# Mixing the streams of a two-layer decoder by finer steps

## Chip, core and metric

The kernel runs on one core of a Trainium2 chip, in one launch. The metric is device time in microseconds (us). Five engines run their own instruction queues side by side: TensorE (PE) multiplies matrices, VectorE (DVE) and ScalarE (ACT) do elementwise work, GpSimd (POOL) adds a few sums of weights, and SyncE (SP) issues nearly all transfers. An instruction starts when those before it on its engine have been issued and the semaphores that it waits for have been reached.

## What is computed

One step of a decoder with two layers, in fp32, for 1024 prompt tokens and 8 sample tokens that share all weights:

```python
for l in range(DEPTH):                       # DEPTH = 2, D_MODEL = 1024, D_FF = 2816
    hn = rmsnorm(h, g[0])
    if l < N_A:                              # layer 0: gated recurrence + memory attention
        mix, S = a_mixer(hn, w_in_a[l], lbs[l], hg_norm[l], mem_k[l], mem_v[l], w_o[l], hg_s0[l])
    else:                                    # layer 1: stick-breaking attention + memory attention
        mix = b_mixer(hn, w_in_b[l - N_A], ..., k_all, v_all, q_pos, k_pos, mem_k[l], mem_v[l], w_o[l])
    h = h + rmsnorm(mix, g[1])
    h = h + rmsnorm(swiglu(rmsnorm(h, g[2]), w_gu[l], w_down[l]), g[3])
    if l == N_A - 1:                         # shared keys and values, after layer 0
        sb_k, sb_v = jnp.split(rmsnorm(h, g_kv) @ w_kv, 2, axis=-1)
```

The samples bring their own recurrent states, paged keys and values, and memory caches; the new states, keys and values are outputs too.

## The kernel before

**Groups and layout.** The tokens are worked in two groups: group 0 has 512 prompt tokens, group 1 has the other 512 and the 8 samples. Activations lie with the features on the partitions and the tokens along the rows, so a projection (`proj`, L212 on) is 8 blocks of 128 features by 512 or 2 x 260 tokens.

**Products in three passes.** A weight tile of 128 x 512 is loaded by SP (L203), its high half is rounded by ACT (L208) and its low half is the difference, taken by DVE (L209). Each 128 x 128 block then takes three matmuls in this order: high weight by high activation, high by low, low by high. So the first two need ACT alone and the third needs DVE. A projection is 48 matmuls (L222) for group 0, twice as many of 260 columns for group 1. `split[0]` always names the last weight split on DVE, and `with tc.issue_after(ins)` keeps what is issued under it behind `ins` on its engine.

**Order.** The program is written as generators, each a stream of steps. `weave((stream, n), ...)` takes the next step from the stream whose count of steps divided by its weight `n` is the smallest; `drain` runs streams to their end. The Tile framework then places each engine's instructions by this order as far as its own scheduling keeps it, and inserts the waits. A stream that waits holds its engine's queue, and all that stands behind it there.

**Buffers.** `mmp` has two pairs of PSUM banks for projections: L247 (first operation of a silu), L414 (adding a partial output to the residual rows) and L818 (gate by up) on DVE free them. `wraw` has 5 raw weight tiles, `wspl` 5 split ones, `cpool` 4 tiles of 128 x 1024, `bpool` 7 of 128 x 512, `apool` 8 of 2 x 520.

**Streams that the change touches.**
- `normed` (L279 on) multiplies the residual rows by the norm, ties each row behind `split[0]`, and splits it. `residual` (L371 on) does the same with a post norm, adds the row of the residual stream and stores it; its first operation (L395) has no tie.
- `kv_proj` projects the shared keys and values; `rows_proj` makes those rows of group 0 that have tokens on the partitions.
- `hgrn_sample` (L1221 on) updates the recurrent states of the samples. It first turns the new values into rows and stores them in DRAM (`vd`), then takes one head a step: it loads the state, broadcasts that head's value rows from `vd` to all partitions (L1239), multiplies and adds (L1253 on), stores the state (L1255), multiplies by the query and sums over partitions by a matmul with `selr` (L1261). In the end the rows go to DRAM and back (`od`, L1269 and L1271) and are transposed (L1274).
- `sample_scores` (L1035 on) takes one sample a step: it loads the keys, broadcasts the query (L1054), multiplies (L1056) and reduces (L1057). `sample_pv` (L1062 on) likewise weights the values (L1077), adds two halves (L1078) and sums them over partitions by a matmul (L1068). Both serve the memory attention (`mem_attn_sample`, transposes L1124 and L1134) and stick-breaking (`sb_sample`).
- Stick-breaking for the prompt makes scores (L1500), runs scans on DVE (L1520), exponentials on ACT (L1523), transposes (L1529) and products with the values (L1540).
- The feed-forward has a plain form (`ffn`, by `proj`) and one by sums of weight quarters (`ffn_w`, L504 and L578, down projection L750 and L782), whose sums of weights (L558 to L565) come from DVE or from sums made ahead (`weight_sums`). Its slices come in parts of 5, 6, 5 and so on. With few free buffers, it takes the raw weight tiles for part 1 from `apool` (L538), where the residual rows of the last output projection lay; `token_rows` (L481) is the last to read those rows, for group 1.

Of the kernel before, what the change touches and what calls it, by code (L numbers as in the profile page):

```python
# [9 lines left out]
F32 = mybir.dt.float32  # L10
# [4 lines left out]
ALU = mybir.AluOpType  # L15
# [8 lines left out]
def tile_decoder(  # L24
# [354 lines left out]
    def residual(g, R, rstd, gc, store, acc=None, first=False):  # L379
        n = NG[g]  # L380
        w = D // 2 if first else n
        ht = [xpool.tile([P, 2, w], F32, tag=f"x{g}", name=nm("ht")) for _ in range(ND // 2)]
        for j in range(ND // 2):
            if first:
                t0 = g * G + j * P
                nc.sync.dma_start(ht[j].rearrange("p a n -> p (a n)"), x_prompt[0, t0 : t0 + P, :])
            else:
                nc.sync.dma_start(ht[j], hs[g][:, 2 * j : 2 * j + 2, :n])
        for k in range(ND):
            if first:  # L390
# [4 lines left out]
            nc.vector.scalar_tensor_tensor(R[k][:, :n], R[k][:, :n], gc(k), rstd[:, :n], op0=ALU.mult, op1=ALU.mult)  # L395
# [263 lines left out]
    class ffn_w:  # L659
# [44 lines left out]
        def part(self, pi):  # L704
# [94 lines left out]
    class ffn:  # L799
# [4 lines left out]
        def part(self, pi, own_silu=False):  # L804
# [5 lines left out]
            for j in range(nf):  # L810
# [225 lines left out]
    def sample_scores(q, load, sc):  # L1036
# [14 lines left out]
        for b in range(NB):  # L1051
# [3 lines left out]
            with tc.issue_after(split[0].ins):  # L1055
                nc.vector.tensor_mul(kt, kt, qb.unsqueeze(1).to_broadcast([P, 2, 512]))  # L1056
            nc.vector.tensor_reduce(  # L1057
                scv[:, :, :, b], kt.rearrange("p k (h d) -> p k h d", h=H), axis=AX.X, op=ALU.add
            )
            yield  # L1060

    def sample_pv(pT, load, xo, k0):  # L1062
# [10 lines left out]
        for b in range(NB):  # L1073
# [4 lines left out]
            nc.vector.tensor_add(vt[:, 0, :], vt[:, 0, :], vt[:, 1, :])  # L1078
# [7 lines left out]
        nc.vector.tensor_copy(ot[:NB, :], po[:NB, :])  # L1086
        pr = S()
# [30 lines left out]
    def mem_attn_sample(l, qm, xo):  # L1118
        HB = H * NB
        sc = small([P, 2 * HB], tag="sc", bufs=2)  # L1120
        yield from sample_scores(qm, mem_loader(cache_mem_k, l), sc)
        pr = S()
# [8 lines left out]
        nc.vector.tensor_scalar(pe[:HB, :NM], pe[:HB, :NM], sm[:HB, 0:1], None, op0=ALU.mult)  # L1131
        pb = S()
# [29 lines left out]
    def rows_proj(W, m0, xt, dst):  # L1162

        pb = [mmp.tile([P, 2, 512], F32, tag="mm", name=nm("mm")) for _ in range(2)]
        for k in range(ND):
# [4 lines left out]
            nc.vector.tensor_sub(ws[:, 1, :], raw, ws[:, 0, :].bitcast(F32))  # L1170
# [50 lines left out]
    def hgrn_sample(Ft, Kt, Qt, vs):  # L1221
# [5 lines left out]
        vd = tc.dram_tile([NB, 512], F32, name=nm("vd"))  # L1227
        nc.sync.dma_start(vd, vT[:NB, :])
        yield
        HB = H * NB  # L1230
# [13 lines left out]
        po = S()  # L1244
        for h in range(H):
# [9 lines left out]
            nc.sync.dma_start(st_sample[0, :, h].rearrange("b k v -> k b v"), stv)  # L1255
            nc.vector.tensor_mul(vbv, stv, col(Qt))
            for a in range(2):
                qs = B(F32R), B(F32R)
                split_to(qs, vb[:, a, :])
                for i, p in enumerate(qs):  # L1260
                    nc.tensor.matmul(  # L1261
                        po[:NB, :], selr[:, 2 * h + a, :], p,
                        start=(h == 0 and a == 0 and i == 0), stop=(h == H - 1 and a == 1 and i == 1),
                    )
            yield
        rows = B()
# [4 lines left out]
        nc.sync.dma_start(ot[:NB, :].rearrange("p (h v) -> p h v", v=P), od.rearrange("h b v -> b h v"))  # L1271
        pr = S()
# [112 lines left out]
    class mixer_a:  # L1385
# [12 lines left out]

        def sample(self):
            yield from hgrn_sample(self.F, self.K, self.Q, self.vs)  # L1400
# [31 lines left out]
    def kv_proj(g, xt):  # L1432
        ks = small([P, 2, H, NB], tag="ks", bufs=1) if g else None
        for j, (out, scr) in enumerate(((sbk_prompt, ksc), (sbv_prompt, vsc))):
            if j and not g:
                rows = [C(), C()]
                yield from rows_proj(w_kv, H * P, xt, rows)
# [24 lines left out]
            for h in range(H):  # L1462
# [106 lines left out]
    def sb_sample(Qs, xo):  # L1569
# [6 lines left out]
        softplus(zb, e, 2 * HB)  # L1576
        cu = S()
# [160 lines left out]
    weave((chain(a1.merge(), a1.mem()), 30), (a1.mem_sample(), 50), (rest(), 24))  # L1738
# [6 lines left out]
    drain(kv_proj(0, xk0))  # L1745
    weave((normed(0, f0.R, f0.r, lambda k: gcol(1, 0, k), xb0), 8), (o1.mm(a1.xo, 7, ND), 1))
# [5 lines left out]
    weave((chain(b0.sb(), b0.mem()), 25), (chain(fw.part(0), fw.part(1)), 18))  # L1752
# [3 lines left out]
    drain(fw.part(3), islice(p4, 4))  # L1756
# [9 lines left out]
    drain(kv_proj(1, xk1))  # L1766
    weave((normed(1, f1.R, f1.r, lambda k: gcol(1, 0, k), xb1), 8), (o0.mm(b0.xo, 7, ND), 1))
# [6 lines left out]
        (chain(b1.sb(), b1.mem()), 40), (chain(b1.sb_sample(), b1.mem_sample()), 39),  # L1774
        (chain(f0.part(0), f0.part(1), f0.part(2), islice(p3, 4)), 30),
# [40 lines left out]
```

## Time and profile before

| | us |
|---|---|
| median of 3 runs | 2419.17 |
| lowest and highest | 2416.83, 2419.40 |
| the profiled execution's own time | 2418.61 |
| its span from first to last instruction | 2416.9 |
| mean granted clock of TensorE in it | 0.999 |

All views below are of that profiled execution. A line such as `PE mm L222 <- DVE t L247: 2.0, 1, 2.0` reads: TensorE's instructions of line 222 that write `mm` waited for DVE's line 247, which writes `t`, for 2.0 us in total, once, 2.0 at the longest. A line of the timeline gives the start, the length to the end of the last of the group, engine, line, operation, output and inputs, shape, count, and in brackets the idle time before it and what ended it. A group of instructions gives count, then busy time, mean duration of one in ns, and idle time before. Matmuls are pipelined, so that their records overlap; what a matmul costs in a row of them is the distance of two starts. "PEld" is the loading of weights, "SPq" the issue of transfers, and the clock is a share of the full one.

### The profile page before, as it was taken

The numbers are of one execution on the slowest core, as the hardware profiler recorded it, in microseconds if no ns is written. First come the engines' busy times: TensorE is split into PE (matmuls) and PEld (weight loads), VectorE is DVE, ScalarE is ACT, GpSimd is POOL, SyncE is SP. The second block draws the span as 40 slices with busy tenths as digits, with TensorE's granted clock in tenths as the row PEclk, the third lists the DMA queues.
The fourth block names the chain that finished last, engine by engine and source line by source line (L and its number), as shares of the span: only waits on it lengthen the run. The fifth ranks groups of instructions, "written<-read, shape, count | busy, mean of one in ns | idle before, by whom it ended". The sixth has DMA issues, their size and how long they took to land. (4 is left out here: it accounts for less than half of the span.)

```text
span 2416.9 us, 41637 instructions
## 1 busy us (share of the span) xinstructions
PE 2384.9 (99%) x15719; PEld 2147.6 (89%) x15719; DVE 1716.2 (71%) x3154; ACT 1271.7 (53%) x2517; POOL 101.9 (4%) x155
## 2 busy tenths in 40 slices
PE   8999999999999999999999999999999999999998
PEld 6888988888779998999999989877777988999998
DVE  5867557675797676878565777788778467776876
ACT  5547544354445554666544554555455446554445
POOL 1000201110000000000000100021000000000000
PEclk9999999999999999999999999999999999999999
DMA  6454766567645447332555546454353243343321
GB/s 190 121 167 118 170 188 158 134 185 195 188 131 152 146 141 218 118 112 76 170 162 150 173 145 190 151 158 150 111 157 120 83 127 118 113 129 100 109 84 67
DMA packets 494987, 342.86 MB, mean 142 GB/s; under 512 B 19469, under 2 KB 446586, under 8 KB 494786
## 3 DMA queue, kind: packets, MB, share of 16 engines
q1 hardware_dynamic: 482242, 306.63, 42.6%
q0 software_dynamic: 12544, 33.56, 5.9%
q8 instruction: 124, 2.03, 0.3%
q14 instruction: 77, 0.63, 0.1%
HBM read 308.18 MB, written 57.10 MB: 151 GB/s over the span
## 5 line engine op out<-in xcount | busy, mean ns | idle before, releaser
L222 PE MATMUL mm<-x,ws 128*128 128x512 f32 (+1 forms) x5208 | 967.9, 343 | 4.5 <-DVE t L247 2.0
L222 PEld LDWEIGHTS mm<-x,ws 128*128 128x128 f32 x5208 | 811.3, 188 | 124.2 <-issue 2.9
L208 ACT CAST ws<-w 128x512 fp32r<-128x512 f32 x612 | 357.5, 586 | 455.8 <-PE mm L222 280.3
L209 DVE TENSOR_TENSOR ws<-w,ws 128x512 fp32r<-128x512 f32 x612 | 392.2, 646 | 246.8 <-ACT ws L208 239.5
L750 PE MATMUL q<-m,ws 128*128 128x260 f32 (+1 forms) x2304 | 282.8, 283 | 0.5 <-ACT m L229 0.3
L750 PEld LDWEIGHTS q<-m,ws 128*128 128x128 f32 x2304 | 277.3, 188 | 2.6 <-ACT m L229 0.8
L578 PE MATMUL q<-y,ws 128*128 128x260 f32 x1824 | 237.5, 284 | 0.7 <-ACT q L585 0.4
L578 PEld LDWEIGHTS q<-y,ws 128*128 128x128 f32 x1824 | 226.0, 188 | 1.9 <-ACT q L589 0.9
L222 PE MATMUL mm<-m,ws 128*128 128x512 f32 x864 | 215.6, 401 | 0.4 <-DVE r L414 0.4
L578 PE MATMUL q<-x,ws 128*128 128x260 f32 (+1 forms) x1548 | 202.9, 283 | 0.0
L222 PEld LDWEIGHTS mm<-m,ws 128*128 128x128 f32 x864 | 160.8, 189 | 36.8 <-DVE r L414 0.7
L578 PEld LDWEIGHTS q<-x,ws 128*128 128x128 f32 x1548 | 192.6, 188 | 0.1
L571 ACT CAST ws<-w 128x512 fp32r<-128x512 f32 x188 | 113.0, 618 | 87.1 <-PE q L750 27.3
L573 DVE TENSOR_TENSOR ws<-w,ws 128x512 fp32r<-128x512 f32 x188 | 126.4, 688 | 37.9 <-ACT ws L571 36.3
L504 PE MATMUL q<-x,ws 128*128 128x260 f32 (+1 forms) x720 | 90.4, 284 | 0.0
L759 DVE TENSOR_TENSOR r<-r,q 128x260 f32<-128x260 f32 (+1 forms) x144 | 54.6, 421 | 48.1 <-PE q L750 47.9
L504 PEld LDWEIGHTS q<-x,ws 128*128 128x128 f32 x720 | 87.8, 188 | 1.0 <-DVE ws L209 0.2
L229 ACT CAST m<-t 128x512 fp32r<-128x512 f32 (+1 forms) x88 | 54.8, 623 | 30.6 <-DVE t L618 15.2
L230 DVE TENSOR_TENSOR m<-t,m 128x512 fp32r<-128x512 f32 (+1 forms) x88 | 60.7, 690 | 12.8 <-ACT m L229 12.1
L277 DVE TENSOR_TENSOR st<-st,n 128x512 f32<-128x512 f32 (+1 forms) x91 | 62.3, 692 | 2.8 <-ACT n L276 1.9
L571 ACT CAST ws<-b 128x512 fp32r<-128x512 f32 x68 | 41.9, 620 | 37.1 <-PE q L750 13.8
L247 DVE TENSOR_SCALAR t<-mm 128x512 f32<-128x512 f32 (+1 forms) x48 | 33.1, 689 | 36.8 <-PE mm L222 36.8
(405 smaller groups left out, 3045.9 us busy)
## 6 DMA issues: line engine op xcount, KB each, us to landing
w<-in_w_gu SPq DMA_DIRECT2D x290, 256.0 KB
w<-in_w_down SPq DMA_DIRECT2D x160, 256.0 KB
w<-in_w_in_a SPq DMA_DIRECT2D x80, 256.0 KB
wsum<-in_w_gu POOLq DMA_DIRECT2D x36, 512.0 KB, 6.3
w<-in_w_o SPq DMA_DIRECT2D x64, 256.0 KB
w<-wsum SPq DMA_DIRECT2D x36, 256.0 KB
w<-in_w_mem_kv SPq DMA_DIRECT2D x32, 256.0 KB
c<-in_cache_mem_k SPq DMA_DIRECT2D x16, 512.0 KB
```

Source lines behind the costliest of these rows:

```text
L208: nc.scalar.copy(ws[:, 0, :n, :], raw[:, :n, :])
L209: split[0] = nc.vector.tensor_sub(ws[:, 1, :n, :], raw[:, :n, :], ws[:, 0, :n, :].bitcast(F32))
L222: nc.tensor.matmul(ps[:, a, : PW[g]], wt, xt[k][:, xi, o : o + PW[g]], start=(k == 0 and wi == 0), stop=(k == nk - 1 and wi == 2),)
L229: nc.scalar.copy(dst[0], src)
L230: nc.vector.tensor_sub(dst[1], src, dst[0].bitcast(F32))
L277: nc.vector.tensor_add(acc[:, :n], acc[:, :n], t[:, :n])
L504: ins = nc.tensor.matmul(pp[a][:, :h], wt, xt[k][:, xi, a * h : (a + 1) * h], start=(k == 0 and wi == 0), stop=(k == ND - 1 and wi == 2),)
L571: nc.scalar.copy(w[:, 0, :], src)
L573: split[0] = nc.vector.tensor_sub(w[:, 1, :], src, w[:, 0, :].bitcast(F32))
L578: nc.tensor.matmul(ps[:, :h], w[:, wj, k * P : (k + 1) * P], x[:, xi, :], start=(first and k == 0 and wi == 0), stop=(k == 3 and wi == 2), ...
L750: nc.tensor.matmul(pp[a][:, :h], wt, mids[k][:, xi, a * h : (a + 1) * h], start=(k == 0 and wi == 0), stop=(k == nf - 1 and wi == 2),)
L759: nc.vector.tensor_add(d, d, pp[a][:, :h])
```

## The change

No matmul, no transfer and no elementwise operation is added or left out; streams are cut into other steps, some instructions are tied behind others, some issue later, and the weights of the mixes follow the new counts of steps.

```diff
-    def normed(g, R, rstd, gc, out, keep=False):
+    def normed(g, R, rstd, gc, out, keep=False, behind=()):
...
-            with tc.issue_after(split[0].ins):
+            with tc.issue_after(behind[k] if behind else split[0].ins):
                 nc.vector.scalar_tensor_tensor(t[:, :n], R[k][:, :n], gc(k), rstd[:, :n], ...)
@@ residual @@
-            nc.vector.scalar_tensor_tensor(R[k][:, :n], R[k][:, :n], gc(k), rstd[:, :n], ...)
+            with tc.issue_after(split[0].ins):
+                nc.vector.scalar_tensor_tensor(R[k][:, :n], R[k][:, :n], gc(k), rstd[:, :n], ...)
@@ ffn_w.part @@
                     if late:
                         drain(late)
-                        yield
+                    yield
                     next(slice_)
                     late = slice_
-                    continue
                 yield
@@ ffn.part @@
+                yield
                 pu = proj(g, w_gu[l], 0, ND, DFF + (f0 + j) * P, self.xt)
@@ sample_scores @@
-            nc.vector.tensor_reduce(scv[:, :, :, b], ...)
+            yield
+            with tc.issue_after(split[0].ins):
+                nc.vector.tensor_reduce(scv[:, :, :, b], ...)
@@ sample_pv @@
-            nc.vector.tensor_add(vt[:, 0, :], vt[:, 0, :], vt[:, 1, :])
+            yield
+            with tc.issue_after(split[0].ins):
+                nc.vector.tensor_add(vt[:, 0, :], vt[:, 0, :], vt[:, 1, :])
...
         nc.vector.tensor_copy(ot[:NB, :], po[:NB, :])
+        yield
         pr = S()
@@ mem_attn_sample @@
         yield from sample_scores(qm, mem_loader(cache_mem_k, l), sc)
+        yield
         pr = S()
...
+        yield
         pb = S()
@@ rows_proj(W, m0, xt, dst, done=None) @@
-            nc.vector.tensor_sub(ws[:, 1, :], raw, ws[:, 0, :].bitcast(F32))
+            split[0] = nc.vector.tensor_sub(ws[:, 1, :], raw, ws[:, 0, :].bitcast(F32))
+            if k % 2 and done is not None:
+                done.append(split[0].ins)
...
-    def hgrn_sample(Ft, Kt, Qt, vs):
+    def value_rows(vs, vd):
         pvv = S()
...
         nc.sync.dma_start(vd, vT[:NB, :])
         yield
+
+    def hgrn_sample(Ft, Kt, Qt, vd):
...
+        late = []
+
+        def total():
+            for h, a, i, p in late:
+                nc.tensor.matmul(po[:NB, :], selr[:, 2 * h + a, :], p, ...)
+            late.clear()
+
         for h in range(H):
...
             nc.sync.dma_start(st_sample[0, :, h].rearrange("b k v -> k b v"), stv)
+            total()
+            yield
             nc.vector.tensor_mul(vbv, stv, col(Qt))
             for a in range(2):
                 qs = B(F32R), B(F32R)
                 split_to(qs, vb[:, a, :])
-                for i, p in enumerate(qs):
-                    nc.tensor.matmul(po[:NB, :], selr[:, 2 * h + a, :], p, ...)
-            yield
+                late.extend((h, a, i, p) for i, p in enumerate(qs))
+            yield
+        total()
...
         nc.sync.dma_start(ot[:NB, :].rearrange("p (h v) -> p h v", v=P), od.rearrange("h b v -> b h v"))
+        yield
+        yield
         pr = S()
@@ kv_proj(g, xt, done), in each projection @@
+                done.append(split[0].ins)
@@ sb_sample @@
         softplus(zb, e, 2 * HB)
+        yield
         cu = S()
...
-    weave((o0.finish(), 17), (chain(a1.v(), a1.qm(A)), 8), (islice(w0, 12), 13))
+    weave((o0.finish(), 17), (chain(a1.v(), a1.rows(), a1.qm(A)), 9), (islice(w0, 12), 13))
-    weave((a1.core(), 22), (f0.part(0), 9), (islice(w0, 16), 17))
+    weave((a1.core(), 22), (f0.part(0), 14), (islice(w0, 16), 17))
-    weave((a1.sample(), 6), (a1.gate(), 4), (f0.part(1), 9), (w0, 9))
+    weave((a1.sample(), 12), (a1.gate(), 4), (f0.part(1), 14), (w0, 9))
-    weave((chain(a1.merge(), a1.mem()), 30), (a1.mem_sample(), 50), (rest(), 24))
+    weave((chain(a1.merge(), a1.mem()), 31), (a1.mem_sample(), 95), (rest(), 33))
-    weave((normed(0, f0.R, f0.r, lambda k: gcol(1, 0, k), xb0), 8), (o1.mm(a1.xo, 7, ND), 1))
+    weave((normed(0, f0.R, f0.r, lambda k: gcol(1, 0, k), xb0, False, done), 8), (o1.mm(a1.xo, 7, ND), 1))
-    weave((chain(b0.sb(), b0.mem()), 25), (chain(fw.part(0), fw.part(1)), 18))
+    weave((chain(b0.sb(), b0.mem()), 25), (chain(fw.part(0), fw.part(1)), 28))
-    drain(fw.part(3), islice(p4, 4))
+    drain(fw.part(3), islice(p4, 8))
...
-        (chain(b1.sb(), b1.mem()), 40), (chain(b1.sb_sample(), b1.mem_sample()), 39),
-        (chain(f0.part(0), f0.part(1), f0.part(2), islice(p3, 4)), 30),
+        (chain(b1.sb(), b1.mem()), 40), (chain(b1.sb_sample(), b1.mem_sample()), 76),
+        (chain(f0.part(0), f0.part(1), f0.part(2), islice(p3, 8)), 48),
...
-    weave((o1.finish(), 17), (chain(p3, f0.part(4, True)), 12))
+    weave((o1.finish(), 17), (chain(p3, f0.part(4, True)), 16))
-    weave((chain(f0.finish(False), store_y(0, f0.R), token_rows(1, o1.R)), 17), (chain(f1.part(0), f1.part(1)), 7))
+    weave((chain(f0.finish(False), store_y(0, f0.R), token_rows(1, o1.R)), 17), (chain(f1.part(0), f1.part(1)), 12))
```

The second group's norm rows (`xb1`) are tied to their `done` in the same way.

More of the change, by code (lines that the diff above doesn't have):

```diff
@@ L1160, in to_token, with rows_proj @@
             )
-    def rows_proj(W, m0, xt, dst):
+    def rows_proj(W, m0, xt, dst, done=None):
         pb = [mmp.tile([P, 2, 512], F32, tag="mm", name=nm("mm")) for _ in range(2)]
@@ L1226, in hgrn_sample @@
         nc.vector.tensor_copy(vT[:NB, :512], pvv[:NB, :])
-        vd = tc.dram_tile([NB, 512], F32, name=nm("vd"))
         nc.sync.dma_start(vd, vT[:NB, :])
         yield
+    def hgrn_sample(Ft, Kt, Qt, vd):
         HB = H * NB
@@ L1244, in hgrn_sample @@
         po = S()
+        late = []
+        def total():
+            for h, a, i, p in late:
+                nc.tensor.matmul(
+                    po[:NB, :], selr[:, 2 * h + a, :], p,
+                    start=(h == 0 and a == 0 and i == 0), stop=(h == H - 1 and a == 1 and i == 1),
+                )
+            late.clear()
         for h in range(H):
@@ L1259, in hgrn_sample @@
                 split_to(qs, vb[:, a, :])
-                for i, p in enumerate(qs):
[L1261 to L1264, printed above, removed]
+                late.extend((h, a, i, p) for i, p in enumerate(qs))
             yield
+        total()
         rows = B()
@@ L1397, in v, with rows @@
             yield from v_proj(self.g, self.W, 8 * P, self.xt, self.V, self.vs)
+        def rows(self):
+            self.vd = tc.dram_tile([NB, 512], F32, name=nm("vd"))
+            yield from value_rows(self.vs, self.vd)
         def sample(self):
-            yield from hgrn_sample(self.F, self.K, self.Q, self.vs)
+            yield from hgrn_sample(self.F, self.K, self.Q, self.vd)
         def core(self):
@@ L1429, in mem_sample, with kv_proj @@
             yield from mem_attn_sample(0, self.Qm, self.xo)
-    def kv_proj(g, xt):
+    def kv_proj(g, xt, done):
         ks = small([P, 2, H, NB], tag="ks", bufs=1) if g else None
@@ L1436, in kv_proj @@
                 rows = [C(), C()]
-                yield from rows_proj(w_kv, H * P, xt, rows)
+                yield from rows_proj(w_kv, H * P, xt, rows, done)
                 for i in range(2):
@@ L1744, in tile_decoder @@
     weave((normed(0, f0.R, f0.r, gkvcol, xk0, True), 8), (o1.mm(a1.xo, 5, 7), 2))
-    drain(kv_proj(0, xk0))
-    weave((normed(0, f0.R, f0.r, lambda k: gcol(1, 0, k), xb0), 8), (o1.mm(a1.xo, 7, ND), 1))
+    done = []
+    drain(kv_proj(0, xk0, done))
+    weave((normed(0, f0.R, f0.r, lambda k: gcol(1, 0, k), xb0, False, done), 8), (o1.mm(a1.xo, 7, ND), 1))
     b0 = mixer_b(0, xb0)
@@ L1765, in tile_decoder @@
     weave((normed(1, f1.R, f1.r, gkvcol, xk1, True), 8), (o0.mm(b0.xo, 5, 7), 2))
-    drain(kv_proj(1, xk1))
-    weave((normed(1, f1.R, f1.r, lambda k: gcol(1, 0, k), xb1), 8), (o0.mm(b0.xo, 7, ND), 1))
+    done = []
+    drain(kv_proj(1, xk1, done))
+    weave((normed(1, f1.R, f1.r, lambda k: gcol(1, 0, k), xb1, False, done), 8), (o0.mm(b0.xo, 7, ND), 1))
     b1 = mixer_b(1, xb1)
```

8 lines of the change are left out of this document (4 added, 4 removed).

## The prediction

> **What bounds the kernel now.** I read the busy times first, then what TensorE waited for, then windows around those waits, then the timeline inside each.
>
> ```profile
> PE 2384.9 (99%) x15719; PEld 2147.6 (89%) x15719; DVE 1716.2 (71%) x3154; ACT 1271.7 (53%) x2517; POOL 101.9 (4%) x155
> ```
>
> TensorE is busy for 2384.9 of 2416.9 us, so 32 us of idle time is nearly all that an edit of order can win. The change adds and drops no matmul; it only moves when the other engines serve TensorE. The waits of TensorE say where the 32 us lie:
>
> ```profile
> PE ns L363 <- DVE xtok L336: 9.4, 2, 7.7
> PE s L1124 <- DVE sc L1057: 2.8, 1, 2.8
> PE mm L222 <- DVE t L247: 2.0, 1, 2.0
> PE s L1529 <- ACT b L1523: 1.7, 7, 0.3
> ```
>
> (Waited for, then us in total, times, longest.) The first 9.4 us are the start of the kernel, which the change leaves alone. The rest is a few single stalls and many small ones. Windows over the stages that the diff touches, and over the 4 us behind the largest stall (length; busy time and instructions of PE, PEld, DVE, ACT, POOL; clock; DMA share; GB/s):
>
> ```profile
> 540.00:562.00 22.00, 20.01 (x110) 16.71 (x109) 15.02 (x20) 7.79 (x14) 4.31 (x4) 1.00 0.91 236
> 640.00:690.00 50.00, 46.23 (x201) 36.32 (x200) 41.99 (x66) 21.88 (x46) 0.00 (x0) 0.97 0.60 171
> 677.00:681.00 4.00, 4.00 (x11) 3.20 (x12) 2.49 (x6) 0.56 (x2) 0.00 (x0) 0.60 0.83 276
> 985.00:1130.00 145.00, 143.92 (x1137) 138.17 (x1136) 117.77 (x241) 92.86 (x201) 0.00 (x0) 1.00 0.35 104
> 1495.00:1506.00 11.00, 9.16 (x75) 8.75 (x73) 11.00 (x19) 5.47 (x10) 0.00 (x0) 1.00 0.54 183
> 1570.00:1805.00 235.00, 231.56 (x1118) 181.89 (x1117) 189.92 (x287) 128.54 (x243) 25.32 (x20) 1.00 0.49 145
> ```
>
> In five of these TensorE is not the only busy engine: DVE works 84% of 640 to 690, all of 1495 to 1506, 81% of 1570 to 1805. The bound is TensorE, interrupted where DVE comes late.
>
> **The change part by part.** Each term is what is taken from or added to the profiled run's time.
>
> *Memory scores of layer 0 (mul and reduce in two steps, yields before the transposes).*
>
> ```profile
> 667.55 0.97 SPq L1054 DMA_DIRECT2D b<-qd  x2
> 669.01 0.62 DVE L1026 TENSOR_SCALAR b<-b,sme 128x256 f32<-128x256 f32 x2
> 671.48 2.36 DVE L1056 TENSOR_TENSOR c<-c,b 128x1024 f32<-128x1024 f32 x2 [0.93 <-DMA b<-qd]
> 673.76 2.34 DVE L1057 TENSOR_REDUCE sc<-c 128x8 f32<-128x1024 f32 x2
> 676.24 0.38 PE L1124 MATMUL s<-ident,sc 128*32 128x128 f32 x2 [2.75 <-DVE sc L1057]
> 677.00 1.22 PE L222 MATMUL mm<-m,ws 128*128 128x512 f32 x2 [0.38 <-DVE r L414]
> ```
>
> The last two samples' products and sums (4.7 us of DVE) stand in one row, TensorE reaches the transposes L1124 at once and idles 2.75 + 0.38 us. The clock row above then shows 0.60 over 4 us: 4 x 0.40 = 1.6 us more. In the built order of the change, four transposes (0.45 us) and 14 matmuls (14 x 0.232 = 3.2 us) stand between the projection that DVE's last drain waits for and L1124, while DVE needs the drain, two small scalings and one reduce: 0.69 + 0.62 + 1.17 = 2.5 us. So 3.1 + 1.6 = 4.7 us go; the new ties put a 0.7 us operation before one drain elsewhere in the stage. I take **-4.0** (between -4.7 and -1.6, if the sums still come late but the clock holds).
>
> *The step from state to output rows.*
>
> ```profile
> 619.10 0.41 PE L1274 MATMUL s<-ident,b 8*128 8x8 f32 x4 [1.16 <-DMA b<-od]
> 546.41 0.37 SPq L1239 DMA_DIRECT2D c<-vd  x1
> ...
> 553.56 1.23 DVE L1253 TENSOR_TENSOR c<-c,a 128x1024 f32<-128x1024 f32 x1 [5.78 <-DMA c<-vd]
> 558.17 0.69 DVE L247 TENSOR_SCALAR t<-mm 128x520 f32<-128x520 f32 x1
> 559.01 3.27 PE L222 MATMUL mm<-x,ws 128*128 128x512 f32 x13 [1.99 <-DVE t L247]
> ```
>
> L1274 waits for a write and a read back; two yields put more than a whole projection (11.1 us) ahead of it: **-1.2** (0 to -1.2). At 546, DVE stands 5.78 us for the broadcast of the values, and behind it stands L247, which frees a PSUM bank: TensorE idles 1.99 us. Storing the value rows earlier doesn't issue the fourth head's broadcast earlier, since SP has it behind the store of a state and a free buffer; but the later half-step takes about half of the work out from in front of L247. **-1.0** (0 to -2.0).
>
> *Residual behind the split (L395).*
>
> ```profile
> 1500.12 2.67 PE L222 MATMUL mm<-x,ws 128*128 128x260 f32 x20 [0.77 <-DVE ws L209]
> 1503.86 2.42 PE L222 MATMUL mm<-x,ws 128*128 128x260 f32 x18 [1.07 <-ACT a L1383]
> ```
>
> Both waits are weight halves or activations queued behind residual and norm rows while DVE is full. With the rows tied behind the split the halves go first: 0.77 + 1.07, **-1.8** (0 to -1.8; what is late next is the row itself, which only the following feed-forward reads).
>
> *Stick-breaking samples (1570 to 1805).* Idle here is 235 - 231.56 = 3.4 us, but overlapping records hide waits inside a run, so I count the matmuls instead.
>
> ```profile
> L222 PE MATMUL mm<-x,ws 128*128 128x512 f32 x504 | 122.2, 397 | 0.0
> L222 PE MATMUL mm<-m,ws 128*128 128x512 f32 x240 | 59.7, 400 | 0.0
> L1540 PE MATMUL s<-b,a 128*128 128x128 f32 x192 | 25.8, 276 | 0.8 <-DVE s L1537 0.8
> L1500 PE MATMUL s<-a,a 128*128 128x512 f32 x36 | 18.6, 598 | 0.0
> L1529 PE MATMUL s<-ident,b 128*128 128x128 f32 x96 | 15.1, 277 | 1.5 <-ACT b L1523 1.3
> ```
>
> Their undisturbed start-to-start times come from the chain and the timeline:
>
> ```profile
> 1772.89 11.12 PE mm L222 x48
> ```
> ```profile
> 1598.84 1.02 PE L1500 MATMUL s<-a,a 128*128 128x512 f32 x2
> 1599.69 0.60 PE L1529 MATMUL s<-ident,b 128*128 128x128 f32 x4
> 1600.13 1.06 PE L1540 MATMUL s<-b,a 128*128 128x128 f32 x8
> 1600.94 7.20 PE L222 MATMUL mm<-m,ws 128*128 128x512 f32 x30
> ```
>
> 744 x 11.12/48 = 172.4; 192 x 0.81/8 = 19.4; 36 x 0.85/2 = 15.3; 96 x 0.44/4 = 10.6; the other 50 at the same rates about 9: 227 of 235 us. Some records may be missing, so of the 8 us I take 6 as lost. A sample's step was 2.4 us of DVE in one piece and becomes two of 1.2; a scan or a drain behind it is late by half as much. But DVE's share stays 81%, and the loads of the values come free later. **-3.5** (-6 to 0).
>
> *Feed-forward with own sums beside stick-breaking (985 to 1130).* Yields after each slice and between gate and up projection only re-mix the streams; 1.1 us is idle. **0** (-1.0 to +2).
>
> *Norm rows tied to `done[k]`.* They now stand among the splits of the key and value projection; a row and its low half (0.69 each) can be ahead of a split, and leave the place behind. **+0.4** (-0.7 to +1.4).
>
> *Last mix (17 to 12).* This one costs. The first weight tiles of part 1 sit in buffers shared with the residual rows of `o1`, which the last token-row transposes (L481) read.
>
> ```profile
> 2118.82 0.60 PE L481 MATMUL s<-ident,a 128*8 128x128 f32 x4
> 2127.48 0.69 DVE L573 TENSOR_TENSOR ws<-w,ws 128x512 fp32r<-128x512 f32 x1 [1.18 <-ACT ws L571]
> 2133.36 1.59 PE L578 MATMUL q<-x,ws 128*128 128x260 f32 x12
> ```
> ```profile
> 763.71 0.37 SPq L538 DMA_DIRECT2D w<-wsum  x1
> 766.51 0.62 ACT L571 CAST ws<-w 128x512 fp32r<-128x512 f32 x1 [0.72 <-DMA w<-wsum]
> ```
>
> Before, 14 us of down projection lie between those transposes and part 1. In the built order of the change, nothing does: L481 twice, then L578. The load is released by the first four and has only the second four, 0.60 us, for cover. Load to cast takes 766.51 - 763.71 = 2.80, the cast 0.62: idle 2.8 us. The low half (0.69) misses the third matmul, due 0.24 after the first, by 0.45, and the next tile, a sum, by about as much: 3.7 us. An idle of 2.75 us preceded the 1.6 us lost to the clock above, one of 1.99 us at 559 none (clock 1.00 in 540 to 562). I take the clock's loss, in part in the shadow of the late halves: **+4.7** (+2.5 to +6.4). Behind this load in SP's queue are the other tiles of part 1; they come 0.4 us apart and are not late by more.
>
> The Trainium skill bears on that term ("TensorE: Matmul & The Clock Gate", "What's actually happening"): it puts the drop to half clock after one idle window of about 3.4 us, and calls the window free-running. Read plainly, 2.8 us would not drop it and the term would be 3.7, the forecast 2411.8; the trace disagrees, with 0.60 after 2.75 us, so the sum keeps 4.7.
>
> **Sum:** -4.0 - 1.2 - 1.0 - 1.8 - 3.5 + 0 + 0.4 + 4.7 = -6.4 us. The profiled execution took 2418.61 us (span 2416.9 and 1.7 around it), 0.56 below the median 2419.17; 2419.17 - 6.4 = **2412.8**.
>
> **The rivals.**
>
> *DVE gets in its own way (slower).* Each tied row must stand behind a split, and a split waits for its cast:
>
> ```profile
> L209 DVE TENSOR_TENSOR ws<-w,ws 128x512 fp32r<-128x512 f32 x612 | 392.2, 646 | 246.8 <-ACT ws L208 239.5
> ```
>
> That is 239.5/612 = 0.39 us a split. The 24 reduces and 24 adds of the samples are newly tied; if each adds one such wait to DVE where it has no room, 48 x 0.39 = 18.7 us, and half reaches TensorE through L247 and L414, it is +9.4, and the -3.5 are not earned: 2412.8 + 12.9 = 2425.7. It decides once DVE passes some 90% in these stages; 81% and 84% now speak against it, the 1495 window at 100% for it.
>
> *The reorder does not reach the stalls (same).* What ends last may be the transfers: 0.93 us before L1056 and 5.78 before L1253 are DMA waits that no yield shortens. Then the 3.5 and 1.0 stay, and the score stall shrinks only by half: 2412.8 + 3.5 + 1.0 + 2.0 = 2419.3. For it: DMA share 0.91 in 540 to 562. Against it: most rows above name DVE or ACT as releaser.
>
> *The late load is covered (faster still).* If the row buffer comes free earlier than the order suggests, the +4.7 go: 2408.1. Against it: the wait stands in the built program.
>
> **How the numbers follow.** The forecast has 0.43 (its own range 2406 to 2418), no reach 0.24, DVE in its own way 0.15, covered load 0.18. No change means within 0.2%, or 4.8 us, about what a measurement of this kernel can tell: 2414.3 to 2424.0. Below lie all of the covered load and some 0.32 of the forecast's 0.43, and 0.06 of no reach: 0.56. Above lie most of DVE's case and a little of the rest: 0.16. Between: 0.28. The best ends of the bounds together give -4.7 - 1.2 - 2.0 - 1.8 - 6 - 1.0 - 0.7 + 2.5 = -14.9, 2404.3; with something below for terms that I missed, 2403. Upward it stops at 2424, which leaves out the half of DVE's case.
>
> **What would show it.** Right: no wait of L1124 on L1057 and no 0.60 clock behind it; L1274 without a wait; the window of the residual above 10.5 us busy of 11; a wait of L578 on ACT L571 of 2.5 to 3.2 us right behind L481, with a clock near 0.6 behind it. Wrong: DVE over 90% busy in the sample stages with L247 or L414 as releasers of TensorE; waits of L1068 or L1077 on `c<-in_cache_mem_v` above 2 us; or L578 starting behind L481 without a gap.

## The result, and the profile after

The changed kernel took 2432.14 us (median of 6 runs, 2430.51 to 2439.99) against 2419.28 us of the kernel before in runs beside it (2416.83 to 2422.16): ratio 1.006, 95% interval 1.005 to 1.007. It is 12.9 us slower, where 6.4 us less was forecast. The profiled execution is the longest of the six, 2439.99 us, with a span of 2438.2. Its mean granted clock is 0.994, against 0.996 of the runs near the median, and by these some 0.002 x 2432 = 4.9 of the 7.9 us between them are clock. Line numbers of the changed kernel are up to 30 higher than before.

Its busy times, and what TensorE waited for:

```profile
PE 2393.2 (98%) x15719; PEld 2155.6 (88%) x15719; DVE 1715.8 (70%) x3153; ACT 1267.0 (52%) x2516; POOL 95.3 (4%) x155
```
```profile
PE ns L363 <- DVE xtok L336: 9.6, 2, 7.7
PE s L1332 <- ACT b L1328: 5.0, 1, 5.0
PE q L579 <- ACT ws L572: 4.5, 4, 3.2
PE s L1567 <- issue: 3.8, 2, 2.2
PE mm L222 <- DVE t L247: 2.7, 1, 2.7
PE q L505 <- DVE r L415: 2.4, 1, 2.4
PE s L1131 <- DVE sc L1060: 1.7, 1, 1.7
```

The work is the same: the same 15719 matmuls. The span of the profiled execution is 21.3 us longer than the one before: TensorE idles 13.0 us more (45.0 for 32.0) and is busy 8.3 us more, most of it at a lower clock, as shown next. Behind the start of the kernel there are now six places where TensorE waits 1.7 us or more in all. Two of them are old: L247, which grew from 2.0 to 2.7, and L1131, which is L1124 of before and shrank from 2.8 to 1.7. The other four are new. Behind each of the six the clock fell. Windows of 4 us behind five stalls and of 8 us behind the sixth (the clock is the third figure from the end):

```profile
402.00:406.00 4.00, 3.54 (x11) 3.43 (x12) 4.00 (x10) 2.45 (x7) 0.08 (x1) 0.57 0.33 93
545.00:549.00 4.00, 3.50 (x17) 3.53 (x18) 2.58 (x5) 3.44 (x6) 0.00 (x0) 0.57 0.83 219
671.50:675.50 4.00, 3.73 (x10) 2.96 (x11) 3.27 (x8) 0.56 (x2) 0.00 (x0) 0.57 0.81 249
722.00:730.00 8.00, 7.24 (x37) 6.95 (x38) 5.82 (x15) 3.26 (x9) 0.00 (x0) 0.57 0.12 35
1774.00:1778.00 4.00, 4.00 (x14) 3.14 (x13) 3.16 (x4) 1.26 (x3) 0.00 (x0) 0.57 0.92 250
2153.00:2157.00 4.00, 3.78 (x20) 3.63 (x19) 2.90 (x5) 2.14 (x5) 0.00 (x0) 0.57 1.04 287
```

Each loses 4 x 0.43 = 1.7 us, the one of 8 us twice that: 11.9 us, against 1.6 at the one place before (677 to 681). The largest stall, from the timeline:

```profile
382.76 0.38 SPq L1276 DMA_DIRECT2D out_st_sample<-c  x1
...
387.78 0.37 SPq L1250 DMA_DIRECT2D c<-in_state_hgrn  x1
...
398.09 1.22 DVE L1273 TENSOR_TENSOR c<-c,a 128x1024 f32<-128x1024 f32 x1 [8.58 <-DMA c<-in_state_hgrn]
399.24 0.68 DVE L247 TENSOR_SCALAR t<-mm 128x512 f32<-128x512 f32 x1
...
402.45 1.00 PE L1332 MATMUL s<-b,a 128*128 128x192 f32 x2 [4.98 <-ACT b L1328]
```

L1273 is a product of the samples' state update. In the text of the program this stream runs in the next mix, and in the kernel before its first products came at 517 us. Here it stands at 398 us in the middle of the prompt's recurrence (L1314 to L1335): its value rows were stored a mix earlier, so nothing but buffers and loads held it back, and the scheduling put it there. The second head's state can be loaded only when the first head's store has freed a buffer; the load is issued at 387.8, and its product starts 10.3 us later. GpSimd loads weight sums in the same stretch, and the DMA engines are 96% busy in it; that this is what makes the load long is not shown (in e9 below the same load takes 7.8 us, at 93%). DVE stands 8.58 us with the drain L247 and the recurrence's own operations behind it, and TensorE 4.98 us behind those.

The other new waits are of the same kind: an operation at the head of DVE's queue that is late, or long, and behind it one that TensorE needs.

```profile
720.02 1.23 DVE L1080 TENSOR_TENSOR c<-c,ss 128x1024 f32<-128x1024 f32 x1 [0.61 <-DMA c<-in_cache_mem_v]
721.16 0.68 DVE L415 TENSOR_TENSOR r<-r,mm 128x512 f32<-128x512 f32 x1
...
721.90 1.50 PE L505 MATMUL q<-x,ws 128*128 128x256 f32 x9 [2.39 <-DVE r L415]
```
```profile
1768.77 1.21 DVE L1060 TENSOR_REDUCE sc<-c 128x8 f32<-128x1024 f32 x1
...
1771.69 0.74 DVE L1542 TENSOR_SCALAR b<-s,biasp 128x512 f32<-128x512 f32 x1
...
1772.54 0.48 DVE L1564 MEMSET s<- 128x512 f32 x1
...
1773.13 1.13 PE L1567 MATMUL s<-b,a 128*128 128x128 f32 x8 [2.22 <-issue]
```

At 720, L415 drains the last projection ahead of the feed-forward with sums, behind a sample's product of 1.23 us that has itself waited 0.61 us for its value load. At 1772, L1564 zeroes the PSUM bank for the next head's products L1567, and stands in DVE's queue behind a sample's reduction and four operations more. The view shows no releaser for the wait ("issue"), but L1567 starts 0.1 us after the zeroing ends, and in the traces of e5 and e10 below the releaser of these products is the zeroing by name. The wait that L1124 had, now of L1131:

```profile
664.18 2.36 DVE L1057 TENSOR_TENSOR c<-c,b 128x1024 f32<-128x1024 f32 x2 [2.06 <-DMA b<-qd]
...
667.06 1.22 DVE L1060 TENSOR_REDUCE sc<-c 128x8 f32<-128x1024 f32 x1
668.19 0.68 DVE L819 TENSOR_TENSOR t<-t,mm 128x512 f32<-128x512 f32 x1
...
670.67 0.38 PE L1131 MATMUL s<-ident,sc 128*32 128x128 f32 x2 [1.67 <-DVE sc L1060]
```

DVE stands 2.06 us for the broadcast of a query, then has two products and a reduction to do before the drain L819, and only behind that the last reduction, for which L1131 waits. Over the whole run DVE's waits for these query broadcasts and for the cached values of the memory samples grew from 7.2 + 2.0 to 11.9 + 9.9 us.

The stall that the forecast did name:

```profile
2148.41 1.03 PE L482 MATMUL s<-ident,a 128*8 128x128 f32 x8
2148.82 5.47 SPq L539 DMA_DIRECT2D w<-in_w_gu  x8
2151.97 0.62 ACT L572 CAST ws<-w 128x512 fp32r<-128x512 f32 x1 [1.88 <-DMA w<-in_w_gu]
...
2152.64 0.50 PE L579 MATMUL q<-x,ws 128*128 128x260 f32 x2 [3.20 <-ACT ws L572]
2153.37 2.54 PE L579 MATMUL q<-x,ws 128*128 128x260 f32 x10 [0.22 <-DVE ws L574]
```

The load is issued in the middle of the last transposes, takes 3.15 us to the cast, and TensorE idles 3.20 us, with the low half 0.22 us late and the clock at 0.57 behind it.

### The profile page after: what moved, and what is told of

Same layout as the page of the kernel before. It is cut to its first block, busy times and chain, and to the rows that moved or that the text cites. A ratio compares the mean times of both kernels' runs of the same rounds, so it can differ in the third digit from the quotient of the medians.

```text
span 2438.2 us, 41599 instructions
## 1 busy us (share of the span) xinstructions
PE 2393.2 (98%) x15719; PEld 2155.6 (88%) x15719; DVE 1715.8 (70%) x3153; ACT 1267.0 (52%) x2516; POOL 95.3 (4%) x155
## 4 chain that ended last, share of the span: by engine, by line
PE 48%; DVE 3%; DMA 2%; ACT 1%; issue 1%; SPq 0%; DVEq 0%; ACTq 0%
PE mm L222 19%; PE q L579 14%; PE q L750 9%; PE s L1567 1%; PE q L782 1%; DMA b<-qd 1%; PE s L1527 1%; PE q L505 1%; PE s L1010 1%; PE s L991 1%; DVE ws L209 0%; PE s L1556 0%; PE ns L1071 0%; DVE c L1057 0%; DVE ws L574 0%
## 5 line engine op out<-in xcount | busy, mean ns | idle before, releaser
L222 PE MATMUL mm<-m,ws 128*128 128x512 f32 x864 | 208.8, 396 | 0.0
L574 DVE TENSOR_TENSOR ws<-b,ws 128x512 fp32r<-128x512 f32 x68 | 46.8, 688 | 19.9 <-ACT ws L572 19.3
```

The source lines that it names most:

```text
L222: nc.tensor.matmul(ps[:, a, : PW[g]], wt, xt[k][:, xi, o : o + PW[g]], start=(k == 0 and wi == 0), stop=(k == nk - 1 and wi == 2),)
L574: split[0] = nc.vector.tensor_sub(w[:, 1, :], src, w[:, 0, :].bitcast(F32))
```

## The experiments

Theory 1: the loss is a few separate stalls, each of an operation that TensorE needs behind a late one in a queue, and each able to cost 3.4 us of half clock too. The rival, here theory 2: the new ties and steps make DVE late all over. All times are medians; ratios and intervals are those on record, estimated from all runs, so that they can differ a little from the quotient of two medians. The kernel before beside them took 2417.97 us (e1 to e4), 2418.92 (e5 to e8), 2418.13 (e9 to e12) and 2418.43 (e13 to e15).

| run | what | us | to before, 95% interval |
|---|---|---|---|
| e1 | changed, state update as before | 2433.0 | 1.0057 (1.0040 to 1.0074) |
| e2 | changed, state update tied | 2423.6 | 1.0022 (1.0012 to 1.0031) |
| e3 | changed, last mix 10 | 2428.4 | 1.0037 (1.0025 to 1.0050) |
| e4 | changed, samples in whole steps | 2435.6 | 1.0072 (1.0056 to 1.0089) |
| e5 | changed, feed-forward steps as before | 2425.5 | 1.0029 (1.0018 to 1.0041) |
| e6 | changed, rows untied | 2432.1 | 1.0058 (1.0041 to 1.0075) |
| e7 | e2 and e3 | 2416.3 | 0.9994 (0.9984 to 1.0004) |
| e8 | e7, zeroes by ACT | 2419.7 | 1.0000 (0.9990 to 1.0009) |
| e9 | before, with the new state update | 2424.3 | 1.0023 (1.0013 to 1.0033) |
| e10 | before, with the samples' two steps | 2421.1 | 1.0010 (1.0000 to 1.0020) |
| e11 | e7, memory samples 80 | 2419.7 | 1.0004 (0.9994 to 1.0013) |
| e12 | e7, memory samples 115 | 2420.2 | 1.0006 (0.9996 to 1.0016) |
| e13 | e7, halves untied | 2416.8 | 0.9989 (0.9980 to 0.9998) |
| e14 | e7, zeroes a step earlier | 2415.7 | 0.9988 (0.9980 to 0.9997) |
| e15 | e13 and e14 | 2417.0 | 0.9995 (0.9986 to 1.0004) |

### The state update: e1, e2, e9

e1 puts `hgrn_sample` of before back, with its weights:

```diff
-    weave((o0.finish(), 17), (chain(a1.v(), a1.rows(), a1.qm(A)), 9), (islice(w0, 12), 13))
+    weave((o0.finish(), 17), (chain(a1.v(), a1.qm(A)), 8), (islice(w0, 12), 13))
-    weave((a1.sample(), 12), (a1.gate(), 4), (f0.part(1), 14), (w0, 9))
+    weave((a1.sample(), 6), (a1.gate(), 4), (f0.part(1), 14), (w0, 9))
```

> The changed kernel with the samples' state update as it was before (value rows, heads in one step, no delayed sums, no yields before its transposes) and the weights of its two mixes with it; all else as changed. Theory 1 (the loss is a few separate stalls, each followed by 3.4 us at half clock): the 4.98 us wait of the prompt's recurrence for ACT and DVE at 402 us, behind a DVE that stands 8.58 us for a state load, goes with its clock loss of 1.6, and so does the 0.7 us by which the wait of L222 for L247 grew and its 1.6 of clock; the 1.2 us wait for the round trip of the output rows comes back: 2432.1 - 7.7 = 2424.4 us. Theory 2 (DVE gets in its own way all over, through the operations tied behind splits): no part gives back more than 3 us, so 2429 to 2433.

Measured: 2433.0, no gain; the number alone lies where theory 2 put it. The wait at 402 us is gone, as is every product of the state update before 500 us. But in the mix in which it now runs, the drain L247 comes later than it did before:

```profile
553.82 1.23 DVE L1263 TENSOR_TENSOR c<-c,a 128x1024 f32<-128x1024 f32 x1 [5.22 <-DMA c<-vd]
...
556.22 0.68 DVE L247 TENSOR_SCALAR t<-mm 128x512 f32<-128x512 f32 x1
...
557.04 3.32 PE L222 MATMUL mm<-x,ws 128*128 128x512 f32 x7 [4.55 <-DVE t L247]
```

DVE waits for the value rows as long as it did before (5.22 and 5.78 us), yet TensorE stands 4.55 us in place of 1.99, with 6.8 us of half clock behind it. In the kernel before TensorE had work for 10.6 us between the issue of that broadcast (546.4) and its wait; here it has 5.7 (from 546.8). That the feed-forward's finer steps moved this work is likely, but was not tested apart. A wait of 2.4 us for the load of `mks` (L1010) with a half clock behind it is new as well, at 648 us. So the old form is no cure, and e1 alone can't say which form is to blame. e2 keeps the new form and takes only the running ahead away:

```diff
-            nc.vector.tensor_mul(stv, stv, col(Ft))
-            nc.vector.tensor_mul(vbv, vbv, col(Kt))
+            with tc.issue_after(split[0].ins):
+                nc.vector.tensor_mul(stv, stv, col(Ft))
+                nc.vector.tensor_mul(vbv, vbv, col(Kt))
```

> The changed kernel with the first two products of each head of the state update tied behind the last weight split, so that they can't run ahead into the prompt's recurrence; nothing else differs. Theory 1: the 4.98 us wait and its half clock go, the wait for L247 at 545 us may stay: 2432.1 - 6.6 = 2425.5. If the hoist is not the cause (theory 2, or the delayed sums and half steps themselves), the time stays within 2430 to 2434.

Measured: 2423.6, so 8.5 less. Neither L1332 nor L247 is among TensorE's waits, and the two half clocks at 402 and 545 us are gone with them. e9 is the test from the other side: the kernel before with this part of the diff and nothing else.

> The kernel before with the state update's part of the change alone (value rows a mix earlier, half steps, delayed sums, two yields, weights 9 and 12 of its mixes). Theory 1 (its operations run ahead into the prompt's recurrence and DVE stands for a state load at the head of its queue): a wait of TensorE of 3 us or more near 400 us and a half clock behind it; 2418.9 + 6.6 + 0.7 - 1.2 = 2425. If the running ahead needs the finer steps of the feed-forward too, no such wait and 2418 or less, as the round trip of the output rows is hidden.

Measured: 2424.3, that is 6.2 more than before. The wait stands where theory 1 puts it, without the finer feed-forward steps (TensorE's waits, then a row of the timeline):

```profile
PE s L1322 <- ACT b L1318: 3.4, 1, 3.4
```
```profile
395.52 1.23 DVE L1263 TENSOR_TENSOR c<-c,a 128x1024 f32<-128x1024 f32 x1 [6.07 <-DMA c<-in_state_hgrn]
```

Added alone it costs 6.2 us, and tied it gives back 8.5: the running ahead is shown as a cause by both. Not all of the 6.2 is this wait: in e9's trace that of L1124 is 3.7 in place of 2.8 us too, and the clock falls at 542 and for 6.8 us at 682.

### The last mix: e3, e7

```diff
-    weave((chain(f0.finish(False), store_y(0, f0.R), token_rows(1, o1.R)), 17), (chain(f1.part(0), f1.part(1)), 12))
+    weave((chain(f0.finish(False), store_y(0, f0.R), token_rows(1, o1.R)), 17), (chain(f1.part(0), f1.part(1)), 10))
```

> The changed kernel with the weight of the last mix 10 in place of 12, which puts 120 down projections between the last token-row transposes and part 1, as before. Theory 1: the wait of 3.2 us for the first weight tile, about 0.9 of late halves behind it and 1.6 of half clock go: 2432.1 - 5.5 = 2426.6, and the profile shows no wait of that product for its cast above 0.3 us and no half clock near 2150 us. Theory 2: the wait goes, but the time moves by less than 3 us.

Measured: 2428.4, 3.8 less, between the two. TensorE goes from the transposes into the down projection and on into part 1 without a gap:

```profile
2122.87 1.04 PE L482 MATMUL s<-ident,a 128*8 128x128 f32 x8
2123.66 14.58 PE L750 MATMUL q<-m,ws 128*128 128x260 f32 x120
2138.07 1.59 PE L579 MATMUL q<-x,ws 128*128 128x260 f32 x12
```

e7 has both mends.

> The changed kernel with both mends: state update tied, last mix 10. If the stalls are separate and add up, -8.5 and -3.8 from 2432.1: 2419.8, equal to the kernel before within 0.2%. If the half clock behind one stall was also paid by another, less: 2422 or more.

Measured: 2416.3, 15.9 less than the changed kernel, where 8.5 + 3.8 = 12.3 were expected from the sum. It is level with the kernel before (interval 0.9984 to 1.0004). With these two causes taken away, the loss is gone. What is left of the change is worth nothing clear of noise, where the forecast had 4.0 + 1.2 + 1.0 + 1.8 + 3.5 - 0.4 = 11.1 us of gain for it.

### The rest of the change: e4, e5, e6, e10

e4 takes the samples' extra steps back (`sample_scores`, `sample_pv`, `mem_attn_sample` and `sb_sample` as before):

```diff
-    weave((chain(a1.merge(), a1.mem()), 31), (a1.mem_sample(), 95), (rest(), 33))
+    weave((chain(a1.merge(), a1.mem()), 31), (a1.mem_sample(), 50), (rest(), 33))
-        (chain(b1.sb(), b1.mem()), 40), (chain(b1.sb_sample(), b1.mem_sample()), 76),
+        (chain(b1.sb(), b1.mem()), 40), (chain(b1.sb_sample(), b1.mem_sample()), 39),
```

> The changed kernel with the samples' score and value steps whole again (product and reduction or addition in one step, no yields before the transposes, weights of the two mixes as before); all else as changed. Theory 1: waits of 1.7 + 0.3 at 670, 2.4 + 0.8 at 720, 1.6 at 1572 and 2.2 at 1773 us go with about 6.4 us of half clock (15.4 in all by the profile), and the waits of the kernel before come back in their places (3.1 + 1.6 at 676 and 6 in the stick-breaking stage): 2432.1 - 4.7 = 2427.4. Theory 2: the ties in these 48 operations are the cause, so this alone gives back 9 us or more: 2423 or less.

Measured: 2435.6, 3.4 more, so both theories missed: in this kernel the two steps are worth 3.4 us, of the 4.0 + 3.5 that the forecast gave the two stages. e10 puts them into the kernel before, with 95 and 76 there:

> The kernel before with the samples' score and value steps of the change alone (two steps each, yields, mix weights 95 and 76; the other streams keep their old steps). Theory 1: the 2.9 us wait at 676 gets shorter and its clock loss may go, the wait of L415 behind a late value load near 710 and of the zeroing near 1560 and 1760 come: the kernel of e4 was 3.4 us slower than the changed one, so about 2418.9 - 3.4 = 2415.5. Theory 2 (the new ties cost): 2423 or more.

Measured: 2421.1, 2.9 more than before, between the two expectations; its interval begins at 1.0000, so this is hardly clear of noise. L1124 waits no more, but at the same place (677 us) TensorE now waits 2.3 us for L414, and 3.5 us for the zeroing L1544 are new. By the medians the worth of these steps has another sign in another mix. e5 undoes the feed-forward's steps, and the weights of its mixes with them, the last mix being back at 7:

```diff
-                yield
                 pu = proj(g, w_gu[l], 0, ND, DFF + (f0 + j) * P, self.xt)
...
                         drain(late)
-                    yield
+                        yield
                     next(slice_)
                     late = slice_
+                    continue
```

> The changed kernel with the feed-forward's steps as before (no yield after every slice, none between gate and up projection) and the weights of its mixes as before (9, 9, 24, 18, 30, 12, 7); all else as changed. Theory 1 (separate stalls): only the last mix's wait goes, as its weight is back at 7 steps of the old length: about -4, 2428. Rival: the finer feed-forward steps are what moved the other streams against each other; then the waits at 397, 542, 719 and 1770 us go too and the time is 2420 or less.

Measured: 2425.5, 6.7 less, between the two. The wait at the last mix is gone (3.8 by e3); the state update still runs ahead (3.4 us at 405). The remaining 2.9 us were not traced to one place. e6 unties the rows:

```diff
-            with tc.issue_after(split[0].ins):
-                nc.vector.scalar_tensor_tensor(R[k][:, :n], R[k][:, :n], gc(k), rstd[:, :n], op0=ALU.mult, op1=ALU.mult)
+            nc.vector.scalar_tensor_tensor(R[k][:, :n], R[k][:, :n], gc(k), rstd[:, :n], op0=ALU.mult, op1=ALU.mult)
...
-    weave((normed(0, f0.R, f0.r, lambda k: gcol(1, 0, k), xb0, False, done), 8), (o1.mm(a1.xo, 7, ND), 1))
+    weave((normed(0, f0.R, f0.r, lambda k: gcol(1, 0, k), xb0), 8), (o1.mm(a1.xo, 7, ND), 1))
...                                          # xb1 likewise
```

> The changed kernel with the residual's first operation not tied and the norm rows of the second layer tied to the last split, as before; all else as changed. Theory 1: the ties of rows removed about 1.2 us (two waits of 0.93 and 1.23 became two of 0.67 and 0.63), so without them 2432 to 2434. Rival (ties behind splits make DVE late): 2428 or less.

Measured: 2432.1, no difference. The ties of rows neither win nor lose.

Taken back one at a time, the parts give back -0.9 (e1), 6.7 (e5, with the last mix), -3.4 (e4) and 0.1 us (e6). That is 2.5 and not 12.9: what a part costs depends on the others beside it, so the figures of single parts are not to be added up.

### The samples' stages: e8, e11 to e15

All start from e7, in whose trace TensorE still waits at 707 us (L415) and for the zeroing at 1555 and 1756.

```diff
# e8
-                nc.vector.memset(po[0], 0.0)
+                nc.scalar.copy(po[0], zcol.to_broadcast([P, 512]))
# e11, e12
-    weave((chain(a1.merge(), a1.mem()), 31), (a1.mem_sample(), 95), (rest(), 33))
+    weave((chain(a1.merge(), a1.mem()), 31), (a1.mem_sample(), 80), (rest(), 33))
+    weave((chain(a1.merge(), a1.mem()), 31), (a1.mem_sample(), 115), (rest(), 33))
# e13, both places
             yield
-            with tc.issue_after(split[0].ins):
-                nc.vector.tensor_reduce(...)
+            nc.vector.tensor_reduce(...)
# e14, in step() of stick-breaking in place of values()
             if old:
                 values(*old)
+            if turned and turned[2] == 0:
+                po[0] = S()
+                nc.vector.memset(po[0], 0.0)
```

> The kernel of e7 with the zeroing of the stick-breaking sums (memset on DVE ahead of the products with the values) done by ACT instead. Theory 1: the waits of 1.6 to 2.4 us before these products near 1560 and 1760 us are for a memset queued on DVE behind a sample's reduction; they go with a half clock of 1.6: e7 less 4 to 5.5, so 2415. If they wait for something else, e7 again.

> The kernel of e7 with the memory samples' weight in their mix 80 in place of 95, so that their steps, and the loads of the caches that these release, lie further apart. Theory 1: at 707 us L415 is late because it stands on DVE behind a product that waits for its value load; with more work between release and use, the DMA wait before that product falls below 0.5 us and the wait of 2.3 + 1.1 goes, 2413; but the stream then ends later than the others, and its last steps have nothing beside them: if this decides, 2418 or more.

> The same with 115: the samples' steps lie closer. The load waits of DVE grow, but they end before the next stage begins, so that its first drain has no sample's product in front. If the place of the wait decides, 2413; if the load waits decide, 2418 or more.

> The kernel of e7 without the ties of the samples' reductions and additions behind the last split; their steps stay two. If the ties are what made DVE late in the samples' stages (the rival of the prediction, 0.39 us for each of 48), the waits at 657, 707, 1555 and 1756 us shrink and the time falls by 4 us or more, to 2412. If the steps' place and the loads decide (theory 1), it stays within 2 us of e7's 2416.3.

> The kernel of e7 with the zeroing of the stick-breaking sums issued one step earlier, still on DVE. Theory 1: the waits of 2.0 and 1.3 us before the products near 1555 and 1756 us, and the half clock behind the first, are for this zeroing in DVE's queue and go: 2416.3 - 4 = 2412. If those products wait for the copy by ACT or the bank, they stay.

> Both of the last two. By theory 1 as e14, 2412; if both count, 2409.

Measured: 2419.7, 2419.7, 2420.2, 2416.8, 2415.7 and 2417.0. None gave the 4 us that theory 1 forecast; e8, e11 and e12 lie 3.4 to 3.9 us above e7. e13 speaks against the rival in these stages: without the ties of the 48 reductions and additions the time is e7's within 0.6 us, where the rival had 4 or more. e14 shows why the zeroing's place brings little. TensorE's waits of e7 first, then of e14:

```profile
PE s L1568 <- issue: 3.0, 2, 1.9
...
PE s L1557 <- ACT b L1551: 1.3, 4, 0.6
```
```profile
PE s L1557 <- ACT b L1551: 5.4, 7, 1.9
```

The wait for the zeroing goes, and the transposes one step on wait for the exponentials, which wait for DVE (L1550, the subtraction behind its scan). e8, which has the zeroing in ACT's queue, moves it to the same place (4.2 us, 7 times). e11 removes the wait of L415 but not the late activations behind it, and has 2.0 us for a cast from 747 us on; e12 makes three of 2.2 to 2.8 us between 635 and 664. In these runs a wait taken from one spot came back at another.

e14 has the lowest median of all: 0.9988 of the kernel before, interval 0.9980 to 0.9997, some 2.8 us faster. It is 16 us faster than the changed kernel. Against the kernel before this is weak: it is the lowest of seven variants with both mends, its interval ends just below 1, and it is 0.6 us from e7.

## Why the prediction was wrong

It forecast 2412.8, within 2403 to 2424, with 0.16 for slower; 2432.14 lies outside. By its own terms:

- **The step from state to output rows (-1.2 and -1.0): wrong, the largest miss.** The round trip is hidden as forecast: no wait on `od` is left. But the argument looked only at the fourth head, of which it says that storing the rows earlier "doesn't issue the fourth head's broadcast earlier", and not at the first heads: with their rows stored a mix earlier they were free to run, and the built order already had their products in front of the recurrence's. It cost +8.5 (e2), or +6.2 alone (e9). DVE stood 8.58 us of a load of 10.3 us; the price of a wait for it at the head of DVE's queue was not in the sum at all. L247 grew by 0.7 instead of halving.
- **The last mix (+4.7): right.** 3.20 us idle (2.8 forecast; the load took 3.15 in place of 2.80 us), 0.22 for the low halves (0.9 forecast), half clock behind; e3 gives 3.8. So the rival of a covered load did not come.
- **Memory scores (-4.0): wrong in the sum.** L1131's wait shrank only from 2.75 to 1.7 us, the clock fell behind it all the same (0.57), and a new wait of 2.4 us for L415 behind a late value load, with two windows of half clock, follows 50 us later. The count of work in front of L1124 left out that DVE comes to its last drain late: it stood 2.06 us for a query broadcast, and the products and the reduction behind that (from 664.18 to 668.19) are ahead of the drain L819.
- **Stick-breaking samples (-3.5): not as forecast.** The order in DVE's queue brought new waits, 1.6 and 2.2 us for the zeroing, which was not looked for; the 6 us taken as lost were a count of matmuls, and no run shows them as waits. e4 puts these steps and those of the memory scores together at -3.4 in this kernel, e10 at +2.9 in the old one.
- **Residual (-1.8) and norm rows (+0.4): no effect in the time.** The waits of 0.77 and 1.07 us are gone, two of 0.51 and 0.47 stand at another place (1448 us), and e6 measures 0.1 in all. The idle time removed was not a time gained.
- **Feed-forward steps (0):** about +2.9 beside the last mix (e5 less e3), and not traced further.
- **The rival of DVE getting in its own way: its mechanism is not what happened.** It named the ties; e13 removes those of the samples and finds nothing. DVE was busy 185.82 of the 235 us from 1580 to 1815, less than before, so DVE did not become the bound. What decided was the order in its queue.
- **The rival of a reorder that does not reach the stalls: nearest in mechanism, not in time.** It named DVE's waits for transfers, which no yield shortens, but priced them as gains that fail to come (2419.3). The runs show them grown and moved: 8.58 us for the state at 398, 2.06 for the query at 664. Of the three signs of being wrong only that of the cached values came (L1080, L1077 of before: 9.9 us in all, 2.0 at the longest).
- **The clock.** The forecast counted one half clock gone and one new. There are six in the profiled execution, one of 6.8 us. By the mean granted clock of the runs (0.9960 of six, 0.9981 of the 31 of the kernel before beside e9 to e12), 0.0021 x 2430 = 5.1 of the 12.9 us are clock, and the rest is left for waits; this is an estimate from clocks given to three places.

The failing step, in one sentence: the sum priced each edit where it had been made and at the stall that it removed, and did not follow what else the freed instructions could now stand in front of.

## What to carry to other kernels

Where instructions are freed from a dependence in a program that a scheduler orders, look in the built order for where they went, and price the wait of the first late load at the head of that queue, together with all that stands behind it. Tie such work behind something of its own stage. In this kernel, with TensorE 99% busy, small waits stand in line: taking one away mostly showed the next. Count an idle time as worth at most its length and the half clock behind it, and test a gain together with the parts that stand beside it.

## What the runs showed of the hardware

The half clock is met more often than the forecast counted, and it goes with much of the spread between runs of one kernel. Among the ten runs of e7 the fastest took 2413.74 us at a mean clock of 1.000, the slowest 2422.70 at 0.996: 0.004 x 2414 = 9.7 us, about their whole distance of 9.0 (the clocks are rounded to 0.001, which is 2.4 us). In the changed kernel's trace it fell behind idle times of 4.98, 2.71, 1.67 + 0.29, 2.39 + 0.76, 2.22 and 3.20 us, but not behind the 1.63 us at 1572:

```profile
1572.00:1576.00 4.00, 3.22 (x18) 2.86 (x19) 3.86 (x7) 2.55 (x6) 1.76 (x2) 1.00 0.58 146
```

In each case it lasted 3.41 us or twice that. The idle time alone does not decide: in e7's trace the clock fell behind a wait of 1.86 us at 1557 and not behind one of 2.16 at 709, and in e13's not behind one of 2.56 at 1762. The length agrees with the window of about 3.4 us that the Trainium skill gives ("TensorE: Matmul & The Clock Gate", "What's actually happening"). That a whole window must be idle doesn't agree: falls stand behind idle times as short as these.
